# A decoder block on one core: five edits to the order of transfers, products and weight splits

## The chip, the cores and the metric

The kernel runs on one core of one Trainium2 chip. The metric is the device time of one execution in microseconds. The engines are PE (matrix products), DVE, ACT and POOL (vector, scalar and general work), and SP, which here only issues transfers.

## The reference

One decoder block over 1024 tokens of width 1024, in float32. The input is normed (`xn`) and multiplied by `w_in`; the result is cut into a pooling input (512), q, k, v (8 heads of 64 each), an indexer's queries, key and head weights, and two sets of 1024 gates:

```
pooled  = trailing means over 2, 4, 8, 16 tokens minus the token, one window per group of 128
mixed   = (pooled per group @ pool_w) * pool_scale ;  y_pool = mixed @ w_pool_proj
scores  = sum over heads of w * relu(iq . ik), causal ; keep the top 256 keys of each query
o       = softmax attention over the kept keys (q, k with partial rope) ;  y_attn = o @ w_attn_proj
merged  = sigmoid(g0) * y_pool + sigmoid(g1) * y_attn ;  h = x + merged @ w_out
a, b    = halves of (causal conv of width 3 over (norm(h) @ w_up) + conv_b), 2816 each
out     = norm(h + (silu(a) * b) @ w_down)
```

## The kernel before, in words

Every float32 product is made of three products of rounded parts: an operand is split into `hi`, a rounded copy (mostly an ACT cast, L48 or L50), and `lo`, the remainder (a subtraction on DVE or POOL, L51), and PE computes hi*hi, hi*lo and lo*hi into one PSUM bank (`mm3`, L85 to L87). A product of 128x128 by 128x512 is PE's unit of work. Tokens are handled in two halves of 512 (`hf`), eight blocks of 128, and input rows in eight chunks `kc` of 128.

Unless a stage is written under `manual_schedule` for an engine, a scheduler orders each engine's instructions by priorities and readiness. Tiles of a pool with the same tag share buffers; pools opened after others close take their space, and an instruction that writes into a reused place waits for the readers of the old tile.

The stages, in order of time:

- **Indexer, gates and pool branch** (`stages`, L187; `pool_branch`, L667). The normed input, transposed and split, is `xT`: two tiles (h and l) for each token half, allocated half 0 first (L195). For each of four groups g the pool branch loads and splits `w_u` and `pool_w`, computes u (48 products), lets DVE form the window sums `s` and the pooled values `pr`, splits them into `ph` and `pl` (one buffer each, L694 and L695; `pl` on POOL), and multiplies them by the mix weights (`pm`, 6 products). The result, split again, goes to DRAM (`mixd`). Eight `gate(c)` with 48 products each follow. The top-k search runs on DVE all the while.
- **q, k, v.** K and Q blocks are projected, roped on DVE, split (`kst`, `qst`) and transposed by PE; then come eight V blocks, which read `xT` last.
- **Attention** (L780 to L908). For units of one block and one head PE, ACT and DVE run in a hand-written order: scores, mask and minimum on DVE, exponentials on ACT, transposes, split of the transposed weights, product with V, evacuation into `ox` (one buffer). Between the units lie the steps of `pool_out` (y_pool, `yp`): it loads `w_pool_proj`, the gates and the four tiles `mx` of mixed values (POOL's queue, L652), one chunk and half at a time. When a block's last head is done, `finish` (L859) brings the two head halves together: per half one transfer `oy<-ox` moves 64 partitions to the other 64 (SP's queue, L871) and one POOL addition forms `ot` (L872); then POOL adds `oy`, multiplies by the reciprocal sums and writes `oT` hi and lo. POOL's queue also issues the loads of q (`qA`, `qB`, L779 to L781).
- **attn_out** (L910). For each half, for each of eight output chunks: load and split `w_attn_proj[c]` (so each chunk's weights twice), load the gate and the pool result, 12 products `ya`, gate and add on DVE, split into `merged`. PE isn't ordered by hand here: the first products with `w_out` (`wo0p`) fill in.
- **mixer_out** (L926), products with `w_out`, residual, norm, transposes into `x2T`.
- **ffn_up** (L983). 22 chunks c of 128 a-columns and 128 b-columns. `plain(c)` (L1027) makes a chunk with 96 products. `pair(c)` (L1092) makes it with seven products of combined quarters, 84 in all, which need the combinations T1 to T4 of the input; DVE forms them (28 operations of 512 columns in each of `sums_1_2` and `sums_3_4`) beside chunks 1 and 2. Chunks 0 to 2 are plain, 3 to 21 pairs. In `plain` the low halves of the b-columns are POOL's (L1033); in `pair` POOL makes the four weight combinations (L1105) and one low half (L1116). `gated` (L1007) runs the convolution on ACT and DVE, and POOL multiplies the two halves (L1019) and issues the store of 512 KB `gd` (L1021).
- **Down-projection and last norm**, untouched.

Of the kernel before, what the change touches and what calls it, by code (L numbers as in the profile page):

```python
# [9 lines left out]
F32 = mybir.dt.float32  # L10
# [5 lines left out]
ALU = mybir.AluOpType  # L16
# [14 lines left out]
NIDX = 584  # L31
WINDOWS = (2, 4, 8, 16)
# [7 lines left out]
class K:  # L40
# [59 lines left out]
    def weights(self, pool, src, shape, tag, name, eng=None, raw_bufs=1, first=None):  # L100
# [4 lines left out]
        hi = pool.tile(shape, F32R, tag=tag + "h", name=name + "h")  # L105
        lo = pool.tile(shape, F32R, tag=tag + "l", name=name + "l")
        self.split(raw, hi, lo, eng, first)
        return hi, lo
# [78 lines left out]
    def stages(self):  # L187
# [7 lines left out]
        xT = [[xt_pool.tile([P, KC, HB], F32R, name=f"xT{n}{hf}") for n in "hl"] for hf in range(2)]  # L195
        self.xT = [list(t) for t in zip(*xT)]
# [19 lines left out]
        self.pool_branch(mx, pl)  # L216
        close()
        ring, close_ring = self.open("ring", "left", bufs=2)
        for c in range(KC):
            self.gate(c)  # L220
# [446 lines left out]
    def pool_branch(self, cd, pool):  # L667
# [3 lines left out]
        nc.sync.dma_start(self.icnt, io["icnt"])  # L671
        for g, w in enumerate(WINDOWS):
# [21 lines left out]
            ph = pool.tile([P, S], F32R, tag="ph", name=f"ph{g}", bufs=1)  # L694
            pl = pool.tile([P, S], F32R, tag="pl", name=f"pl{g}", bufs=1)  # L695
            self.split(pr, ph, pl, gp)
            for hf in range(2):
                cs = slice(hf * HB, (hf + 1) * HB)
                pm = self.bank("mm", f"pm{g}_{hf}")
                self.mm3(pm, pwh, pwl, ph[:, cs], pl[:, cs], True, True)  # L700
                hi, lo = (cd.tile([P, HB], F32R, tag=f"mixed{n}", name=f"mixed{n}{g}{hf}") for n in range(2))
                nc.scalar.activation(hi, pm, AF.Copy, scale=self.psc[:, g:g + 1])
                nc.vector.scalar_tensor_tensor(lo, pm, self.psc[:, g:g + 1], hi.bitcast(F32),
                                               op0=ALU.mult, op1=ALU.subtract)
                nc.sync.dma_start(self.mixd[0, hf, :, g, :], hi.bitcast(F32))
                nc.sync.dma_start(self.mixd[1, hf, :, g, :], lo.bitcast(F32))
# [61 lines left out]
    def attention(self, pool, fq, yp):  # L768
# [90 lines left out]
        def finish(i):  # L859
# [9 lines left out]
            for o in range(2):  # L869
                mine, other = slice(o * DH, (o + 1) * DH), slice((1 - o) * DH, (2 - o) * DH)  # L870
                nc.sync.dma_start(oy[mine], ox[other, :, o, 0:P])  # L871
                nc.gpsimd.tensor_tensor(ot[mine], ox[mine, :, o, 0:P], ox[mine, :, o, P:2 * P], op=ALU.add)  # L872
# [37 lines left out]
    def attn_out(self, pool):  # L910
        nc, io = self.nc, self.io
        xh, xl = [[self.oT[n][:, :, hf * HB:(hf + 1) * HB] for hf in range(2)] for n in range(2)]
        for hf in range(2):
            for c in range(KC):
                cs = slice(hf * HB, (hf + 1) * HB)
                wh, wl = self.weights(pool, io["w_attn_proj"][c], [P, 4, P], "wa", f"wa{c}_{hf}", raw_bufs=3)
                g1 = pool.tile([P, HB], F32, tag="g1", name=f"g1l{c}_{hf}", bufs=3)
                nc.sync.dma_start(g1, self.g[KC + c][:, cs])
                m0 = pool.tile([P, HB], F32, tag="m0", name=f"m0l{c}_{hf}", bufs=3)
                nc.sync.dma_start(m0, self.m0[c][:, cs])  # L920
                ps = self.fm_half("mm", f"ya{c}_{hf}", wh, wl, xh, xl, 4, hf)
                nc.vector.tensor_tensor(g1, ps, g1, op=ALU.mult)
                nc.vector.tensor_tensor(m0, m0, g1, op=ALU.add)
                self.split(m0, self.merged[hf][0][:, c, :], self.merged[hf][1][:, c, :])
# [58 lines left out]
    def ffn_up(self, fw, pool, wx, x2_last, close_h):  # L983
# [19 lines left out]
        def halves(t, src, eng):  # L1003
            nc.scalar.copy(t[:, 0], src)  # L1004
            eng.tensor_tensor(t[:, 1], src, t[:, 0].bitcast(F32), op=ALU.subtract)  # L1005

        def gated(c, H):  # L1007
# [11 lines left out]
            nc.gpsimd.tensor_tensor(b, a, b, op=ALU.mult)  # L1019
# [67 lines left out]
        with self.tc.manual_schedule(engines=PE):  # L1087
            plain(1, sums_1_2)
            plain(2, sums_3_4)
        T = {n: [t[:, 0], t[:, 1]] for n, t in T.items()}  # L1090

        def pair(c):  # L1092
# [23 lines left out]
            operand_of(4, A[1, 1], nc.gpsimd)  # L1116
# [30 lines left out]
        with self.tc.manual_schedule(engines=PE):  # L1147
            for c in range(3, NF):
                pair(c)
# [305 lines left out]
```

## Time and profile before

| | us |
|---|---|
| median of three runs | 1511.73 (1511.61 to 1514.7) |
| profiled execution | 1508.14 |
| its span, first to last instruction | 1506.4 |
| mean granted TensorE clock | 0.981 |

[...] In the table by stage (rows 3 below) the columns are: the stretch, its length, busy us with the number of instructions for PE, PEld (weight loads), DVE, ACT and POOL, the granted clock, the busy share of the 16 DMA engines, and GB/s. Attention lies from 508.9 to 681.1, attn_out from 686 to 752, the first four chunks of the up-projection from 842 to about 930. In a timeline "[6.25 <-DMA mx<-mixd]" means that the engine was idle for 6.25 us before the instruction and that this transfer ended it. A product of 128x512 is shown with 0.39 us although the next begins earlier: products are pipelined, so PE's rate is read from the distance of starts.

### The profile page before, as it was taken

What the parts mean: (1) busy time and instruction counts of PE and PEld (TensorE: products, weight loads), DVE (VectorE), ACT (ScalarE), POOL (GpSimd) and SP (SyncE); (2) the same over time, 40 slices, a digit from 0 to 9 for tenths busy, and PEclk for the clock granted to TensorE, in tenths of its full rate; (3) what the DMA queues carried; (4) which work ended last, traced back from release to release, by engine and by line L of the source; (5) the groups of instructions that cost most, each with busy time, mean ns of one, the idle gap of its engine ahead of it and who ended that gap; (6) DMA issues with size and microseconds to landing.
All of it is one profiled execution on the core that took longest, in us unless ns stands there. A gap on an engine that the chain in (4) does not pass through costs nothing.

```text
span 1506.4 us, 18703 instructions
## 1 busy us (share of the span) xinstructions
PE 1421.1 (94%) x6682; PEld 1176.5 (78%) x6682; DVE 1151.2 (76%) x1909; ACT 650.0 (43%) x1117; POOL 487.2 (32%) x358
## 2 busy tenths in 40 slices
PE   5999999999889799998899997999999999999997
PEld 4888877887678578886688786888888888888886
DVE  7756999999981156786716878888888888949897
ACT  7656222213333255883402444444444445444353
POOL 4102423213342255534300247555555553100000
PEclk9999999999989899999999998999999999999999
DMA  9002513422013465217621213222222221875663
GB/s 339 15 22 69 161 63 107 140 77 70 29 56 112 161 195 168 71 29 240 228 112 78 93 70 126 85 84 84 84 84 98 84 85 42 306 281 182 239 200 126
DMA packets 74061, 184.46 MB, mean 122 GB/s; under 512 B 8560, under 2 KB 13552, under 8 KB 73456
## 3 DMA queue, kind: packets, MB, share of 16 engines
q1 hardware_dynamic: 65360, 159.16, 30.5%
q0 software_dynamic: 8608, 24.12, 4.7%
q8 instruction: 52, 0.85, 0.2%
q14 instruction: 41, 0.34, 0.1%
HBM read 140.25 MB, written 40.89 MB: 120 GB/s over the span
## 4 chain that ended last, share of the span: by engine, by line
PE 62%; DVE 24%; DMA 5%; issue 3%; ACT 3%; POOL 2%; SPq 0%; ACTq 0%; DVEq 0%; POOLq 0%
DVE tk_junk L563 11%; PE up L85 8%; PE up L87 8%; PE up L86 8%; PE d L87 5%; PE d L86 5%; PE d L85 5%; PE o L844 2%; PE pt L827 2%; DVE tk_r L575 1%; DVE tk_cand L576 1%; PE is L448 1%; PE is L447 1%; PE wvp L87 1%; PE wvp L85 1%
## 5 line engine op out<-in xcount | busy, mean ns | idle before, releaser
L563 DVE TENSOR_SCALAR_CACHE_REDUCE tk_junk<-score,tk_cand 128x384 bf16<-128x384 f32 (+1 forms) x186 | 175.1, 941 | 1.8
L1014 DVE SCALAR_TENSOR_TENSOR acc<-H,cw,acc 128x1023 f32<-128x1023 f32 x88 | 133.2, 1530 | 20.7 <-ACT acc L1012 19.9
L85 PE MATMUL up<-T,w 128*128 128x512 f32 x304 | 118.6, 390 | 0.3 <-ACT w L1004 0.3
L87 PE MATMUL up<-T,w 128*128 128x512 f32 x304 | 118.4, 389 | 0.1
L86 PE MATMUL up<-T,w 128*128 128x512 f32 x304 | 118.3, 389 | 0.0
L85 PE MATMUL d<-op 128*128 128x512 f32 x292 | 113.6, 389 | 0.0
L86 PE MATMUL d<-op 128*128 128x512 f32 x292 | 113.6, 389 | 0.0
L87 PE MATMUL d<-op 128*128 128x512 f32 x292 | 113.6, 389 | 0.0
L1005 DVE TENSOR_TENSOR w<-s,w 128x512 fp32r<-128x512 f32 x76 | 89.4, 1178 | 26.1 <-ACT w L1004 25.8
L1019 POOL TENSOR_TENSOR acc<-acc,acc 128x1024 f32<-128x1024 f32 x22 | 69.8, 3173 | 93.2 <-ACT w L1004 59.7
L1005 POOL TENSOR_TENSOR w<-upr,w 128x512 fp32r<-128x512 f32 x25 | 43.6, 1748 | 135.4 <-DVE w L1005 97.4
L85 PE MATMUL up<-x2T,w 128*128 128x512 f32 x200 | 79.4, 397 | 5.5 <-ACT r L1127 3.2
L1004 ACT CAST w<-s 128x512 fp32r<-128x512 f32 x76 | 47.2, 621 | 80.7 <-PE up L87 80.6
L87 PE MATMUL up<-x2T,w 128*128 128x512 f32 x200 | 79.1, 395 | 0.0
L86 PE MATMUL up<-x2T,w 128*128 128x512 f32 x200 | 79.0, 395 | 0.0
L834 DVE TENSOR_TENSOR PT<-pt,PT 128x512 fp32r<-128x512 f32 (+3 forms) x96 | 50.5, 554 | 29.9 <-ACT PT L833 29.3
L1012 ACT ACTIVATE acc<-H,cb,cw 128x1024 f32<-128x1024 f32 x44 | 54.8, 1245 | 36.8 <-DVE H L1144 23.0
L85 PEld LDWEIGHTS up<-T,w 128*128 128x128 f32 x304 | 57.2, 188 | 12.5 <-ACT w L1004 0.8
L87 PEld LDWEIGHTS up<-T,w 128*128 128x128 f32 x304 | 57.1, 188 | 12.5 <-DVE w L1005 0.5
L1004 ACT CAST w<-upr 128x512 fp32r<-128x512 f32 x69 | 42.1, 618 | 56.9 <-PE up L87 47.5
L86 PEld LDWEIGHTS up<-T,w 128*128 128x128 f32 x304 | 57.2, 188 | 11.9
L85 PEld LDWEIGHTS d<-op 128*128 128x128 f32 x292 | 54.8, 188 | 11.5
(862 smaller groups left out, 4171.8 us busy)
## 6 DMA issues: line engine op xcount, KB each, us to landing
upr<-w_up SPq DMA_DIRECT2D x44, 512.0 KB, 4.1
rawg<-gd SPq DMA_DIRECT2D x37, 512.0 KB, 5.5
raww<-w_down SPq DMA_DIRECT2D x33, 512.0 KB, 5.3
gd<-acc POOLq DMA_DIRECT2D x22, 512.0 KB, 3.1
g<-gt SPq DMA_DIRECT2D x32, 256.0 KB, 2.0
xb<-x SPq DMA_DIRECT2D x8, 512.0 KB, 5.6
xTr<-xT SPq DMA_DIRECT2D x8, 512.0 KB, 6.6
mixd<-mixed SPq DMA_DIRECT2D x16, 256.0 KB, 3.0
```

Source lines behind the costliest of these rows:

```text
L85: t.matmul(ps, sh, mh, start=start, stop=False, skip_group_check=onto)
L86: t.matmul(ps, sh, ml, start=False, stop=False, skip_group_check=onto)
L87: t.matmul(ps, sl, mh, start=False, stop=stop, skip_group_check=onto)
L563: nc.vector.tensor_scalar(junk[:, :W], self.score[b], thr, None, op0=ALU.is_ge, op1=ALU.add, accum_out=cnt[:, j:j + 1])
L827: nc.tensor.transpose(pt[:, j - j0, :], t[:, j * P:(j + 1) * P], self.ident)
L834: nc.vector.tensor_tensor(PT[:, j0:j1, 1, :], pt[:, 0:j1 - j0, :], PT[:, j0:j1, 0, :].bitcast(F32), op=ALU.subtract)
L844: nc.tensor.matmul(live[k]["o"][:, h % 2, :], self.V[:, j, h, :], live[k]["PT"][:, j].rearrange("p a t -> p (a t)"), start=j == 0, stop=j ...
L1004: nc.scalar.copy(t[:, 0], src)
L1005: eng.tensor_tensor(t[:, 1], src, t[:, 0].bitcast(F32), op=ALU.subtract)
L1012: nc.scalar.activation(a, H[o], AF.Identity, bias=cb[:, n:n + 1], scale=cw[:, n, 2:3])
L1014: nc.vector.scalar_tensor_tensor(a[:, d:], H[o][:, 0:S - d], cw[:, n, 2 - d:3 - d], a[:, d:], op0=ALU.mult, op1=ALU.add)
L1019: nc.gpsimd.tensor_tensor(b, a, b, op=ALU.mult)
```

## The change

Five edits:

- `xT` is allocated half 1 first.
- The pool branch becomes a generator: the mix of group g is issued after u of group g+1, the last one after `gate(0)`; `ph` and `pl` get two buffers; PE's order in pool branch and gates is fixed as written.
- `oy<-ox` is issued from POOL's queue.
- `attn_out` runs over pairs of chunks, inside them over halves, inside these over the two chunks; each chunk's weights are loaded and split once and kept (four buffers of hi and lo).
- `PLAIN = 4`: chunk 3 is plain, pairs begin at 4. In plain chunks DVE makes all low halves and the product of the two halves; in the first pair DVE makes the combinations and the low half that were POOL's. The `gd` store stays on POOL's queue.

```diff
-        xT = [[xt_pool.tile([P, KC, HB], F32R, name=f"xT{n}{hf}") for n in "hl"] for hf in range(2)]
-        self.xT = [list(t) for t in zip(*xT)]
+        xT = {hf: [xt_pool.tile([P, KC, HB], F32R, name=f"xT{n}{hf}") for n in "hl"] for hf in (1, 0)}
+        self.xT = [list(t) for t in zip(xT[0], xT[1])]
...
-        self.pool_branch(mx, pl)
-        close()
-        ring, close_ring = self.open("ring", "left", bufs=2)
-        for c in range(KC):
-            self.gate(c)
+        with tc.manual_schedule(engines={mybir.EngineType.PE}):
+            branch = self.pool_branch(mx, pl)
+            next(branch)
+            self.gate(0)
+            for _ in branch:
+                pass
+            close()
+            ring, close_ring = self.open("ring", "left", bufs=2)
+            for c in range(1, KC):
+                self.gate(c)
...
-            ph = pool.tile([P, S], F32R, tag="ph", name=f"ph{g}", bufs=1)
-            pl = pool.tile([P, S], F32R, tag="pl", name=f"pl{g}", bufs=1)
+            ph = pool.tile([P, S], F32R, tag="ph", name=f"ph{g}", bufs=2)
+            pl = pool.tile([P, S], F32R, tag="pl", name=f"pl{g}", bufs=2)
             self.split(pr, ph, pl, gp)
...
+            mixed.append((g, pwh, pwl, ph, pl))
+            if g:
+                mix(*mixed.pop(0))
+        yield
+        mix(*mixed.pop(0))
...
-                nc.sync.dma_start(oy[mine], ox[other, :, o, 0:P])
+                nc.gpsimd.dma_start(oy[mine], ox[other, :, o, 0:P])
...
-        for hf in range(2):
-            for c in range(KC):
-                cs = slice(hf * HB, (hf + 1) * HB)
-                wh, wl = self.weights(pool, io["w_attn_proj"][c], [P, 4, P], "wa", f"wa{c}_{hf}", raw_bufs=3)
...
+        w = {}
+        for c0 in range(0, KC, 2):
+            for hf in range(2):
+                for c in (c0, c0 + 1):
+                    cs = slice(hf * HB, (hf + 1) * HB)
+                    if hf == 0:
+                        w[c] = self.weights(pool, io["w_attn_proj"][c], [P, 4, P], "wa", f"wa{c}", raw_bufs=3, bufs=4)
+                    wh, wl = w[c]
...
-            nc.gpsimd.tensor_tensor(b, a, b, op=ALU.mult)
+            (nc.vector if c < PLAIN else nc.gpsimd).tensor_tensor(b, a, b, op=ALU.mult)
...
-                    halves(w[o, k], raw[:, o, 4 * k:4 * k + 4], nc.gpsimd if o else nc.vector)
+                    halves(w[o, k], raw[:, o, 4 * k:4 * k + 4], nc.vector)
...
             plain(2, sums_3_4)
+            for c in range(3, PLAIN):
+                plain(c)
...
-                nc.gpsimd.tensor_tensor(t, a, b, op=op)
+                (nc.gpsimd if c > PLAIN else nc.vector).tensor_tensor(t, a, b, op=op)
...
-            operand_of(4, A[1, 1], nc.gpsimd)
+            operand_of(4, A[1, 1], nc.gpsimd if c > PLAIN else nc.vector)
...
-            for c in range(3, NF):
+            for c in range(PLAIN, NF):
                 pair(c)
```

`mix` holds the lines L697 to L706 unchanged. The rest of the kernel is as before.

## Rows read from the trace of the kernel before

**Rows 1.** Part 1 of the page: busy us, share and instructions.

```profile
PE 1421.1 (94%) x6682; PEld 1176.5 (78%) x6682; DVE 1151.2 (76%) x1909; ACT 650.0 (43%) x1117; POOL 487.2 (32%) x358
```

**Rows 2.** Waits of PE: line, releaser: us in total, times, longest.

```profile
PE yp L85 <- DMA mx<-mixd: 6.2, 1, 6.2
PE pm L85 <- ACT ph L50: 5.5, 2, 3.3
PE ya L85 <- ACT wa_0h L50: 5.3, 1, 5.3
PE up L85 <- DVE u L1134: 4.5, 2, 4.1
...
PE up L85 <- ACT r L1127: 3.2, 1, 3.2
```

**Rows 3.** Table by stage, columns as named in the profile section.

```profile
225.00:275.00 50.00, 46.56 (x192) 37.55 (x191) 49.79 (x94) 14.02 (x21) 19.26 (x11) 0.94 0.31 103
...
350.00:434.40 84.40, 71.55 (x338) 57.29 (x336) 83.45 (x185) 29.57 (x55) 38.29 (x26) 0.97 0.17 51
...
508.90:522.20 13.30, 4.86 (x13) 3.56 (x13) 1.26 (x6) 1.80 (x7) 4.83 (x7) 0.62 1.01 381
522.20:681.10 158.90, 152.95 (x977) 133.61 (x975) 110.12 (x252) 112.33 (x265) 78.62 (x88) 1.00 0.40 116
...
700.00:753.00 53.00, 46.33 (x181) 34.02 (x182) 42.63 (x55) 22.85 (x40) 18.49 (x14) 0.97 0.75 247
...
911.00:950.00 39.00, 31.25 (x115) 23.99 (x114) 31.34 (x29) 17.01 (x25) 24.52 (x16) 0.87 0.39 144
950.00:1275.00 325.00, 325.00 (x1435) 269.12 (x1434) 268.96 (x257) 147.19 (x202) 169.72 (x116) 1.00 0.22 80
```

**Rows 4.** Timeline of PE, 506 to 523 us: start, us, instruction, idle before.

```profile
508.63 0.27 PE L800 MATMUL s<-kstack,qB 128*128 128x128 f32 x1
515.15 0.76 PE L85 MATMUL yp<-mx,wph 128*128 128x512 f32 x1 [6.25 <-DMA mx<-mixd]
...
522.24 0.22 PE L799 MATMUL s<-kstack,qA 128*128 128x128 f32 x1
```

**Rows 5.** Timeline of POOL, 430 to 535 us.

```profile
508.81 2.17 POOL L652 DMA_DIRECT2D mx<-mixd  x4 [23.91 <-PE s L800]
```

**Rows 6.** The tile mx: landing of its four transfers, 1 MB each.

```profile
DMA to landing us min/median/max: 6.2/9.9/13.2
```

**Rows 7.** Timeline of DVE and POOL, 835 to 950 us.

```profile
844.02 1.25 DVE L75 TENSOR_TENSOR h7u<-h7u,h7t 128x1 f32<-128x1 f32 x1
...
847.68 0.68 DVE L1005 TENSOR_TENSOR w<-upr,w 128x512 fp32r<-128x512 f32 x1
...
880.66 12.35 POOL L1019 TENSOR_TENSOR acc<-acc,acc 128x1024 f32<-128x1024 f32 x1 [6.69 <-DVE acc L1014]
...
931.48 2.67 POOL L1019 TENSOR_TENSOR acc<-acc,acc 128x1024 f32<-128x1024 f32 x1 [1.87 <-issue]
```

**Rows 8.** Timeline of PE, 672 to 754 us.

```profile
686.40 0.76 PE L85 MATMUL ya<-oT,wa_0h 128*128 128x512 f32 x1 [5.27 <-ACT wa_0h L50]
...
751.83 0.39 PE L85 MATMUL wo0p<-wo0a,merged 128*128 128x512 f32 x1
```

**Rows 9.** Groups by line, DVE, 686 to 753 us: busy us, mean ns.

```profile
L51 DVE TENSOR_TENSOR wa_1l<-wa_1r,wa_1h 128x512 fp32r<-128x512 f32 x8 | 9.6, 1205 | 0.9 <-ACT wa_1h L50 0.9
```

**Rows 10.** DMA issues: queue, count, KB each, median us to landing.

```profile
qB<-qd POOLq DMA_DIRECT2D x32, 128.0 KB, 3.6
...
oy<-ox SPq DMA_DIRECT2D x16, 128.0 KB, 3.2
```

**Rows 11.** The tile qB: issues on POOL, duration ns min/median/max, first and last start.

```profile
L780 POOL DMA_DIRECT2D qB<-qd x16: 523/539/614, 477.8 to 640.1; - x16
```

**Rows 12.** Timeline of PE and POOL, 205 to 290 us.

```profile
220.15 0.39 PE L85 MATMUL u<-xTh,wu2h 128*128 128x512 f32 x1
...
223.64 2.39 POOL L51 TENSOR_TENSOR pl<-pr,ph 128x1024 fp32r<-128x1024 f32 x1 [0.93 <-ACT ph L50]
```

More of the change, by code (lines that the diff above doesn't have):

```diff
@@ L31 @@
 NIDX = 584
+PLAIN = 4
 WINDOWS = (2, 4, 8, 16)
@@ L98, in feature_major, with weights @@
                 t.matmul(ps[:, hf, :], wl[:, kc, :], xh[hf][:, kc, :], start=False, stop=last)
-    def weights(self, pool, src, shape, tag, name, eng=None, raw_bufs=1, first=None):
+    def weights(self, pool, src, shape, tag, name, eng=None, raw_bufs=1, first=None, bufs=2):
         nc = self.nc
@@ L104, in weights @@
         nc.sync.dma_start(raw, src)
-        hi = pool.tile(shape, F32R, tag=tag + "h", name=name + "h")
-        lo = pool.tile(shape, F32R, tag=tag + "l", name=name + "l")
+        hi = pool.tile(shape, F32R, tag=tag + "h", name=name + "h", bufs=bufs)
+        lo = pool.tile(shape, F32R, tag=tag + "l", name=name + "l", bufs=bufs)
         self.split(raw, hi, lo, eng, first)
@@ L671, in pool_branch, with mix @@
         nc.sync.dma_start(self.icnt, io["icnt"])
+        mixed = []
+        def mix(g, pwh, pwl, ph, pl):
+            for hf in range(2):
+                cs = slice(hf * HB, (hf + 1) * HB)
+                pm = self.bank("mm", f"pm{g}_{hf}")
+                self.mm3(pm, pwh, pwl, ph[:, cs], pl[:, cs], True, True)
+                hi, lo = (cd.tile([P, HB], F32R, tag=f"mixed{n}", name=f"mixed{n}{g}{hf}") for n in range(2))
+                nc.scalar.activation(hi, pm, AF.Copy, scale=self.psc[:, g:g + 1])
+                nc.vector.scalar_tensor_tensor(lo, pm, self.psc[:, g:g + 1], hi.bitcast(F32),
+                                               op0=ALU.mult, op1=ALU.subtract)
+                nc.sync.dma_start(self.mixd[0, hf, :, g, :], hi.bitcast(F32))
+                nc.sync.dma_start(self.mixd[1, hf, :, g, :], lo.bitcast(F32))
         for g, w in enumerate(WINDOWS):
@@ L693, in pool_branch @@
                                            op0=ALU.mult, op1=ALU.subtract)
-            ph = pool.tile([P, S], F32R, tag="ph", name=f"ph{g}", bufs=1)
-            pl = pool.tile([P, S], F32R, tag="pl", name=f"pl{g}", bufs=1)
+            ph = pool.tile([P, S], F32R, tag="ph", name=f"ph{g}", bufs=2)
+            pl = pool.tile([P, S], F32R, tag="pl", name=f"pl{g}", bufs=2)
             self.split(pr, ph, pl, gp)
-            for hf in range(2):
-                cs = slice(hf * HB, (hf + 1) * HB)
[L699 to L706, printed above, removed]
+            mixed.append((g, pwh, pwl, ph, pl))
[3 more added lines that the diff above has]
+        mix(*mixed.pop(0))
     def load_w(self, pool, src, dst, name):
@@ L912, in attn_out @@
         xh, xl = [[self.oT[n][:, :, hf * HB:(hf + 1) * HB] for hf in range(2)] for n in range(2)]
-        for hf in range(2):
-            for c in range(KC):
-                cs = slice(hf * HB, (hf + 1) * HB)
-                wh, wl = self.weights(pool, io["w_attn_proj"][c], [P, 4, P], "wa", f"wa{c}_{hf}", raw_bufs=3)
[L917 to L924, printed above, removed]
+        w = {}
+        for c0 in range(0, KC, 2):
+            for hf in range(2):
+                for c in (c0, c0 + 1):
+                    cs = slice(hf * HB, (hf + 1) * HB)
+                    if hf == 0:
+                        w[c] = self.weights(pool, io["w_attn_proj"][c], [P, 4, P], "wa", f"wa{c}", raw_bufs=3, bufs=4)
+                    wh, wl = w[c]
+                    g1 = pool.tile([P, HB], F32, tag="g1", name=f"g1l{c}_{hf}", bufs=3)
+                    nc.sync.dma_start(g1, self.g[KC + c][:, cs])
+                    m0 = pool.tile([P, HB], F32, tag="m0", name=f"m0l{c}_{hf}", bufs=3)
+                    nc.sync.dma_start(m0, self.m0[c][:, cs])
+                    ps = self.fm_half("mm", f"ya{c}_{hf}", wh, wl, xh, xl, 4, hf)
+                    nc.vector.tensor_tensor(g1, ps, g1, op=ALU.mult)
+                    nc.vector.tensor_tensor(m0, m0, g1, op=ALU.add)
+                    self.split(m0, self.merged[hf][0][:, c, :], self.merged[hf][1][:, c, :])
     def mixer_out(self, pool, r1, hp):
```

## The prediction

> **What bounds the kernel now.** I read the page's busy shares first: TensorE works 94% of the span [rows 1], so only its gaps and its slow stretches can give anything. The waits of PE say who ends those gaps [rows 2], and the table by stage says where they lie and whether the clock fell there [rows 3]. Its last row is the yardstick: in the steady part of the up-projection 1435 products fill 325.00 us, 0.2265 us each at a granted clock of 1.00. Four stages fall short of it: the start of attention (PE busy 4.86 of 13.3 us, clock 0.62), the output products (46.33 of 53, 0.97), the first chunks of the up-projection (31.25 of 39, 0.87), and the two stages beside the top-k search, where DVE is full (49.79 of 50 and 83.45 of 84.4) and PE isn't [rows 3]. The change touches all of these. The profiled execution took 1508.14 us (span 1506.4), 3.6 us under the median of 1511.73; I make the sum against 1508.1 and add 3.6 at the end. A measurement of this kernel can tell about 0.2%, 3 us, from no change.
>
> **A. The two halves of xT change places.** The last product before attention starts at 508.63; then PE waits until 515.15 for the mixed values, once more a little later, runs its first twelve yp products at the lower clock, and goes on with scores at 522.24 [rows 4]. The four transfers of mixed values are issued by POOL at 508.81, after 23.91 us in which it waited for PE, so it had been free since 484.9 [rows 5]. They need 6.2 to 9.9 us to land (minimum and median) [rows 6]. They wait because their tiles, with those of w_pool_proj and of the first gates, take the space of xT's second half, which the last V products still read. Allocated in the other order, that space holds half 0, whose last reader is V block 3 of 8; four blocks of 24 products at 0.2265 follow it, so it is free 21.7 us earlier, and even the median landing fits in twice. Half 1 then lies where the attention output goes, which is written much later. What is late next is the first softmax: scores, exponentials and the split of the last V block had 13 us of cover and then have 2.7. Without the wait 522.24 - 508.9 = 13.3 us become 12 x 0.2265 = 2.7: a gain of 10.6. Bounds: 10.6, and 7 if block 0's exponentials are late. I take **-10.0**.
>
> **B. Four plain chunks, POOL idle beside them.** The fourth chunk is computed with 96 products in place of 84: 12 x 0.2265 = +2.7 on PE. In its place disappears the first pair's stall: PE waits 4.5 on u (4.1 of it once) and 3.2 on r1 [rows 2], and the clock of 0.87 over 39 us costs 0.13 x 39 = 5.1 [rows 3]; together 12.8. Why DVE is late there shows when POOL runs beside it. A one-column DVE operation takes 1.25 us while POOL splits weights, a 512-column one 0.68 alone; POOL's product takes 12.35 us in the middle of DVE's sums and 2.67 later [rows 7]. The edit moves to DVE: two low halves for each of four chunks (8 x 0.68 = 5.4), four products of a and b, five operations of the next pair (3.4), and it drops about nine 512-column operations of the pair replaced (-6.1). No row shows the 1024-column product on DVE: from below twice 0.68, from above POOL's 2.67; I take 1.36 as DVE's own rate, 5.4 for four. DVE gets 8 us more in some 105, where it now has idle time (31.34 busy of 39 [rows 3]), and is spared the operations stretched by POOL. The transfers of the gated product stay on POOL, now behind DVE. The T sums get one chunk more of time (some 21.7 us of PE) before a pair needs them. Ends: -12 (all 12.8 and half the opening stall, less 2.7) and +3 (the stall only moves to the next pair). I take **-8**, a gap of 2 us left.
>
> **C. attn_out two chunks at a time.** From 686.40 to 751.83 PE runs 192 ya and 24 wo0p products [rows 8]: 65.4 us for 216 x 0.2265 = 48.9, 16.5 lost. Removed: eight loads of 256 KB with their SP issues, eight ACT casts, and eight DVE splits, which take 1.2 us here and 0.68 where nothing is beside them [rows 7, 9], together 5.4 to 9.6 of DVE's work; it has 42.63 in 53 us [rows 3]. PE's waits here are mostly for DVE. The half-0 results now come spread over the stage, so the scheduler has less of wo0p to fill gaps with; that work is only moved. The beginning stays: the 5.3 us for the first weight cast [rows 2] may go, but the low part needs DVE and space that block 7 of attention frees, so I count nothing. DVE's saving does not go over to PE in full. Ends: -13 (all but the cold start) and +1. I take a third of the loss, **-5.5**.
>
> **D. Attention's swapped halves go by POOL's queue.** 16 transfers of 128 KB move from SP, where they land in 3.2 us, to POOL; the nearest row is qB, the same size on POOL's queue in the same stage: 3.6 us [rows 10], 0.54 us of POOL each to issue [rows 11]. That is 16 x 0.54 = 8.6 us of POOL, which has 78.62 of 158.9 [rows 3]. POOL's own order puts the second transfer behind the first add (1.28 us), so it goes out 1.2 us later than now, and the block's end and the release of its ox by 1.6. PE runs 152.95 of 158.9 there [rows 3], so there are other products to hide it. SP no longer stands behind attention, and the first weights may be fetched earlier. Ends: -2, and 8 blocks x 1.6 = +13 with nothing hidden. I take **+0.5**.
>
> [...] The rows show 16 qB issues between 523 and 614 ns with DVE busy beside them [rows 11]. [...]
>
> **E. Pool branch in a fixed PE order.** Products of the mix weights come one group later, after the next group's u. Now the scheduler puts them between; PE waits 5.5 for ph in two places [rows 2] and has clock 0.94 in 50 us (3 lost) [rows 3]. With the fixed order m0 follows u1, whose last product ends at about 220.2, while POOL finishes pl at 223.64 + 2.39 = 226.0 [rows 12]: a wait of 5.9. If all four groups did so, 4 x 5.9 = 23.6, less the 5.5, +18. But DVE, not PE, sets the end of k and q: from 350 to 434.4 PE idles 12.85 us beside a full DVE [rows 3], so a delay up to that is absorbed there. Ends: -8 (all waits and slow clock gone) and +18. I take **+1**.
>
> **Sum:** -10.0 - 8 - 5.5 + 0.5 + 1 = -22.0; 1508.1 - 22.0 = 1486.1, and 3.6 more, in terms of the median, **1489.7**. From here on times are medians.
>
> **Rivals.**
> 1. The fixed order's waits aren't absorbed: +18 in place of +1, 1506.7. For it: DVE's own chain leads to ph. Against it: DVE has other work to do meanwhile. Chance 0.14.
> 2. DVE becomes the bound in B and C: the plain chunk costs its 2.7 and C gives 0, so 1511.7 - 10 + 2.7 + 1.5 = 1505.9. For it: DVE at 31.34 of 39 and 42.63 of 53 before it gets POOL's work. Against it: the stretched operations of [rows 7]. Chance 0.14.
> 3. The mixed values don't move: POOL's queue still has something before them that waits for V. Then -22 + 10 = -12, 1499.7. For it: POOL issues in order, and a transfer of q precedes them. Against it: POOL was idle for 23.91 us with nothing else to wait for [rows 5]. Chance 0.07.
> 4. **Slower:** POOL's queue starves in attention. If issues beside DVE stretch as POOL's product does [rows 7], 12.35 / 2.67 = 4.6 times, each goes from 0.54 to 2.5, two per block are 3.9 more, with the 1.6 of D 5.5 per block, 44 in eight; 1489.7 + 44 - 0.5 = 1533. It decides from 22.5 / 8 = 2.8 us per block that PE really waits. For it: the block's ox has one buffer. Against it: [rows 11]. [...] Chance 0.09.
> Two of the first three together come out near no change: 0.06. The forecast as summed, 1480 to 1497, has 0.50.
>
> **Numbers.** Faster: 0.50 + 0.14 + 0.14 + 0.07 = 0.85; same 0.06; slower 0.09. The low end takes C at -11 and B at -12, about 12 under the forecast, 1478; the high end takes in rivals 1 to 3, 1507. Outside lie the slower case, the middle and a little below.
>
> **What would show it.** A: the mixed values issued about 487, no PE gap near 509, the clock 1.00 there. B: no wait on u or r1, one chunk more of plain products, POOL without operations before the first pair but the transfers of gd, DVE's 512-column operations at 0.7 throughout. C: eight loads of w_attn_proj, the stage nearer 60 than 65 us. D: sixteen oy on POOL's queue landing at about 3.6, PE's wait on ox still near 3. E: waits on pl after u1, u2 and u3, and the k and q stages ending near 434. I am wrong if PE's waits move to ox, if k's end slides past 440, or if the first yp still waits for its transfer.

## The result, and the profile after

The changed kernel takes 1491.06 us (median of four executions, 1490.35 to 1494.92) beside 1511.67 for the kernel before on the same chip: ratio 0.9868, 95% interval 0.9843 to 0.9892. That is 20.6 us less; 1489.7 was forecast.

The profiled execution after has a span of 1493.2 us, the profiled one before 1506.4. They differ by 13.2, not by 20.6, so the stages have to be read one by one. The table gives, for every kernel of this study, distances in us between starts on PE, each worked out from the tiles' rows of that kernel's trace, which give tenths, so that a distance is good to 0.1: from the start of the span to the first u product; on to the first V product; from the first score product to the scores behind the first yp group; on to the last transpose of the sums (attention); on to the first wo1p product (attn_out and what fills it); from the first up product to the first down product. The stretches left out are the same within 0.4 us (V 45.4, the second half of w_out 52.5), but for the end (219.3 to 220.4).

| kernel | start to u | u to V | first yp | attention | attn_out | up | span |
|---|---|---|---|---|---|---|---|
| before | 198.4 | 264.5 | 13.9 | 158.7 | 109.0 | 444.7 | 1506.4 |
| changed | 203.2 | 270.0 | 3.2 | 158.1 | 106.8 | 434.6 | 1493.2 |
| e1_noE | 203.7 | 264.0 | 3.2 | 157.5 | 105.7 | 433.4 | 1484.8 |
| e2_noC | 202.4 | 268.8 | 3.2 | 159.7 | 109.0 | 433.7 | 1495.1 |
| e3_noD | 203.8 | 270.0 | 3.2 | 159.3 | 104.0 | 433.7 | 1491.6 |
| e4_Aonly | 198.5 | 264.7 | 3.2 | 158.1 | 109.3 | 444.8 | 1495.9 |
| e5_plain3 | 198.4 | 268.9 | 3.2 | 159.5 | 105.4 | 432.4 | 1485.1 |
| e6_poolon | 198.5 | 269.3 | 3.2 | 157.7 | 107.7 | 437.8 | 1491.5 |
| e7_early | 202.2 | 265.6 | 3.2 | 157.7 | 104.3 | 433.4 | 1483.6 |
| e8_mixlater | 200.7 | 263.7 | 3.2 | 159.8 | 107.1 | 432.2 | 1483.9 |
| e9_best | 202.1 | 264.4 | 3.2 | 157.8 | 104.5 | 432.4 | 1481.5 |
| e10_start | 202.3 | 264.3 | 16.8 | 160.9 | 107.7 | 444.6 | 1513.9 |
| e11_bestnoD | 202.1 | 264.2 | 3.2 | 158.6 | 102.0 | 432.4 | 1479.6 |
| e12_start2 | 201.9 | 263.4 | 3.2 | 160.1 | 103.1 | 432.3 | 1481.2 |

Between the first two lines lie -10.7 at the first yp group, -10.1 in the up-projection, -2.8 in attention and attn_out together, and, against the change, +5.5 between u and V and +4.8 before any line that the change touches. The last is not the change's: e5_plain3 and e6_poolon have all that code and begin with 198.4 and 198.5.

The timeline of the changed kernel answers to [rows 4, 5]:

```profile
497.27 2.17 POOL L660 DMA_DIRECT2D mx<-mixd  x4 [2.06 <-PE wvp L89]
...
518.86 0.27 PE L817 MATMUL s<-kstack,qB 128*128 128x128 f32 x1
518.97 0.45 PE L87 MATMUL yp<-mx,wph 128*128 128x512 f32 x1
...
521.77 0.22 PE L816 MATMUL s<-kstack,qA 128*128 128x128 f32 x1
```

POOL now waits for a V product in the middle of that stage, 21.6 us ahead of the last score product; PE goes from it to yp without a gap, and the twelve products take 2.80 us, from 518.97 to 521.77, at a granted clock of 1.00.

The table by stage for the first chunks of the up-projection. First a line of the kernel before, which goes with the sixth of [rows 3]:

```profile
840.00:911.00 71.00, 67.92 (x297) 55.49 (x296) 59.95 (x83) 33.24 (x53) 32.17 (x12) 0.98 0.17 61
```

Then the same two stretches of the changed kernel:

```profile
840.00:911.00 71.00, 71.00 (x307) 58.32 (x306) 63.59 (x97) 35.47 (x55) 1.48 (x2) 0.96 0.23 83
911.00:950.00 39.00, 39.00 (x174) 32.30 (x173) 24.10 (x26) 15.61 (x24) 13.01 (x10) 1.00 0.26 95
```

PE is full in both, at a clock of 1.00 (the profile gives it as a share of full speed) in the second, where it had 31.25 busy at 0.87; DVE is busy for 63.59 + 24.10 = 87.7 us in the two stretches, before 59.95 + 31.34 = 91.3, although it has taken over POOL's part; POOL does almost nothing in the first. The stretches don't hold quite the same work: the changed up-projection begins 3.2 us earlier and has no pair at chunk 3. The comparison with the same chunks is that of e6_poolon, below.

The waits of PE, changed kernel:

```profile
PE pm L87 <- ACT ph L52: 6.9, 3, 3.3
PE pm L88 <- POOL pl L53: 6.6, 4, 1.9
PE ya L89 <- DVE wa0l L53: 4.6, 1, 4.6
...
PE up L87 <- DVE u L1157: 0.4, 1, 0.4
```

Against [rows 2] the waits for mx and r1 are gone and that for u is 0.4; the mix products now wait 13.5 us in place of 5.5; and the wait at the start of attn_out has only changed its name, from the first cast (the high part of the weights) to their first low part.

### The profile page after: what moved, and what is told of

The parts are those of the page before. It is cut to its first block, busy times and chain, and to the rows that moved or that the text cites. A ratio compares the mean times of both kernels' runs of the same rounds, so it can differ in the third digit from the quotient of the medians.

```text
span 1493.2 us, 18608 instructions
## 1 busy us (share of the span) xinstructions
PE 1418.0 (95%) x6694; PEld 1177.1 (79%) x6694; DVE 1137.0 (76%) x1909; ACT 646.0 (43%) x1108; POOL 446.7 (30%) x354
## 4 chain that ended last, share of the span: by engine, by line
PE 68%; DVE 22%; DMA 3%; ACT 3%; issue 3%; POOL 1%; SPq 0%; ACTq 0%; DVEq 0%; POOLq 0%
DVE tk_junk L571 11%; PE up L87 9%; PE up L88 9%; PE up L89 9%; PE d L87 5%; PE d L88 5%; PE d L89 5%; PE o L861 2%; PE pt L844 2%; DVE tk_r L583 2%; DVE tk_cand L584 1%; PE is L456 1%; PE is L455 1%; PE wvp L87 1%; PE wvp L88 1%
## 5 line engine op out<-in xcount | busy, mean ns | idle before, releaser
L1035 DVE SCALAR_TENSOR_TENSOR acc<-H,cw,acc 128x1023 f32<-128x1023 f32 x88 | 129.4, 1484 | 15.8 <-ACT acc L1033 15.1
L87 PE MATMUL up<-T,w 128*128 128x512 f32 x288 | 112.0, 389 | 0.0
L88 PE MATMUL up<-T,w 128*128 128x512 f32 x288 | 112.0, 389 | 0.0
L89 PE MATMUL up<-T,w 128*128 128x512 f32 x288 | 112.0, 389 | 0.0
L1026 DVE TENSOR_TENSOR w<-s,w 128x512 fp32r<-128x512 f32 x72 | 82.5, 1146 | 34.8 <-ACT w L1025 34.5
L87 PE MATMUL up<-x2T,w 128*128 128x512 f32 x208 | 82.4, 396 | 2.3 <-ACT w L1025 2.3
L88 PE MATMUL up<-x2T,w 128*128 128x512 f32 x208 | 82.1, 395 | 0.0
L89 PE MATMUL up<-x2T,w 128*128 128x512 f32 x208 | 82.1, 395 | 0.0
L1040 POOL TENSOR_TENSOR acc<-acc,acc 128x1024 f32<-128x1024 f32 x18 | 49.2, 2733 | 80.8 <-ACT w L1025 52.2
L1042 POOL DMA_DIRECT2D gd<-acc x22 | 16.4, 747 | 161.2 <-DVE acc L1040 160.3
L89 PEld LDWEIGHTS d<-op 128*128 128x128 f32 x292 | 54.8, 188 | 11.5
L87 PEld LDWEIGHTS d<-op 128*128 128x128 f32 x292 | 54.8, 188 | 11.5
L88 PEld LDWEIGHTS d<-op 128*128 128x128 f32 x292 | 54.8, 188 | 11.2
L87 PEld LDWEIGHTS up<-T,w 128*128 128x128 f32 x288 | 54.1, 188 | 11.3
```

Source lines behind the costliest of these rows:

```text
L87: t.matmul(ps, sh, mh, start=start, stop=False, skip_group_check=onto)
L88: t.matmul(ps, sh, ml, start=False, stop=False, skip_group_check=onto)
L89: t.matmul(ps, sl, mh, start=False, stop=stop, skip_group_check=onto)
L1035: nc.vector.scalar_tensor_tensor(a[:, d:], H[o][:, 0:S - d], cw[:, n, 2 - d:3 - d], a[:, d:], op0=ALU.mult, op1=ALU.add)
L1040: (nc.vector if c < PLAIN else nc.gpsimd).tensor_tensor(b, a, b, op=ALU.mult)
```

## The experiments

All edits are against the changed kernel unless said otherwise. Times are medians, ratios are to executions of the kernel before on the same chip, whose median was 1510.2 to 1512.4. The kernels ran on several chips, so between chips the ratios are compared and not the medians; most intervals overlap, and it is the distances in the table that tell the edits apart. "..." in a diff marks lines left out.

**e1_noE.** Pool branch and gates as before:

```diff
-        with tc.manual_schedule(engines={mybir.EngineType.PE}):
-            branch = self.pool_branch(mx, pl)
...
+        self.pool_branch(mx, pl)
+        close()
+        ring, close_ring = self.open("ring", "left", bufs=2)
+        for c in range(KC):
+            self.gate(c)
...
```

The lines left out put the mix back into its group, with one buffer each for ph and pl.

> The changed kernel with pool branch and gates as before (no fixed order of PE, mix weights in the same group). Theory 1: the fixed order costs; in the two profiles the stretch from the first u product to the first V product is 264.5 us before and 270.0 after, so it goes back to 264 to 265, and the median falls by 4 to 6 from 1491 to about 1486. Rival: DVE's top-k search sets the end of the stretch and the 5.5 us belong to that one execution, which started late; then the stretch differs by less than 2 and the median stays within 2 of 1491. My forecast had +1 for this part.

Measured: 1487.06, ratio 0.9836 (0.9815 to 0.9857), u to V 264.0. The fixed order costs: in the five kernels that have it as the change made it the stretch is 268.8 to 270.0, in the eight with the order of before 263.4 to 265.6.

**e2_noC.** `attn_out` as before:

```diff
-        w = {}
-        for c0 in range(0, KC, 2):
-            for hf in range(2):
-                for c in (c0, c0 + 1):
...
+        for hf in range(2):
+            for c in range(KC):
...
+                wh, wl = self.weights(pool, io["w_attn_proj"][c], [P, 4, P], "wa", f"wa{c}_{hf}", raw_bufs=3)
...
```

> The changed kernel with attn_out as before: two passes, weights loaded and split twice. Theory 1: from the transposes of the last block's sums to the first wo1p product it was 109.4 us before and 107.2 after, so the part is worth about 2: 1493. Rival, my forecast: 5.5, so 1496 to 1497. A third: the gain of 2 comes from SP's freedom and not from this part; then the stretch stays at 107 and the time at 1491.

Measured: 1497.09, ratio 0.9898 (0.9877 to 0.9919); attn_out 109.0, exactly what it was. The third theory is out. The stretch is 2.2 longer and the median 6 higher; the medians can't tell 2 from 5, and the next run shows that the size depends on the queue of the oy transfers.

**e3_noD.** The transfers back on SP:

```diff
-                nc.gpsimd.dma_start(oy[mine], ox[other, :, o, 0:P])
+                nc.sync.dma_start(oy[mine], ox[other, :, o, 0:P])
```

> The changed kernel with the oy transfers back on SP's queue. Theory 1: attention's stretch is 0.5 us longer (158.2 against 157.7) and the first products of attn_out, which began 4 us earlier after attention, begin later again, but the first product with the low part stays at 7.2 us after the last transposes, since its split waits for ox either way: 1491 to 1492. Rival: the early fetch of weights is worth its 4 us: 1495. Second rival, the slower case of my forecast: POOL's queue costs in attention, and without it the stretch is shorter by 3 or more: 1488 or less.

Measured: 1492.91, ratio 0.987 (0.9848 to 0.9893): no difference from the change. But inside, attention is 1.2 longer and attn_out 2.8 shorter, 104.0, the first product with a low part again at the same distance from the last transposes (6.7 against 6.8). The timeline of PE at the start of attn_out, changed kernel first:

```profile
681.41 0.47 PE L87 MATMUL ya<-oT,wa0h 128*128 128x512 f32 x1 [1.28 <-ACT wa0h L52]
...
686.69 0.79 PE L89 MATMUL ya<-oT,wa0l 128*128 128x512 f32 x1 [4.58 <-DVE wa0l L53]
```

and e3_noD:

```profile
687.25 0.77 PE L87 MATMUL ya<-oT,wa0h 128*128 128x512 f32 x1 [5.30 <-ACT wa0h L52]
```

With SP free the first product comes 4 us earlier (681.41 is 1.6 us after the last transpose, with SP's queue it is 5.6), but PE gets only two products out of it and then waits 4.58 for the low part. With SP's queue PE waits 5.30 once.

**e4_Aonly.** The kernel before with the halves of xT exchanged and nothing else:

```diff
-        xT = [[xt_pool.tile([P, KC, HB], F32R, name=f"xT{n}{hf}") for n in "hl"] for hf in range(2)]
-        self.xT = [list(t) for t in zip(*xT)]
+        xT = {hf: [xt_pool.tile([P, KC, HB], F32R, name=f"xT{n}{hf}") for n in "hl"] for hf in (1, 0)}
+        self.xT = [list(t) for t in zip(xT[0], xT[1])]
```

> The kernel before with only the two halves of xT exchanged. Theory 1: from the first score product to the second group of scores it takes 3.2 us in place of 13.9, and the whole gains that, 10.7: 1511.7 becomes 1501. Rival: part of it comes back as waits in attention for the first softmax or for later gates, and the median is 1503 to 1506. Second rival: the gain needs POOL's or SP's queue as in the whole change, and the mixed values still come late: 1511.

Measured: 1497.88, ratio 0.9913 (0.9894 to 0.9931), 14.5 under the kernel before; first yp 3.2, nothing given back in attention (158.1). This edit alone carries over half of the change. The median falls by more than the 10.7 of the two profiles. A possible reason, not shown by a run of its own, is in e10_start, which lacks the edit too and whose profiled execution was the slowest of its twelve: there the first yp group took 16.8 us. Without the edit the wait depends on how long four transfers of 1 MB take (6.2 to 13.2 us in the kernel before, 8.3 to 15.2 in e10_start); with it they take 6.3 to 14.7 and the distance is 3.2 in all twelve traces.

**e5_plain3.** `PLAIN = 4` becomes `PLAIN = 3`, DVE keeps POOL's work.

> The changed kernel with pairs from chunk 3 again, but DVE still does the work of POOL in plain chunks and in the first pair. From the first up product to the first down product it took 444.7 us before and 434.6 changed. Theory 1: the stretch is mostly DVE stretched by POOL, so without POOL the pair at chunk 3 is nearly free of waits, and the 12 products of the plain chunk (2.7 us) are saved: 432 to 435, median 1489 to 1491. Rival: the fourth plain chunk gives the sums the time they need; without it the pair waits as before, and the stretch is 440 or more, median 1496 or more.

Measured: 1488.01, ratio 0.9861 (0.9837 to 0.9885), up 432.4, the shortest but for e8_mixlater's 432.2, and the same in e9, e11 and e12, which have it too. The wait for u is 1.5 us there, so some of the pair's stall is left. With four plain chunks and DVE doing POOL's work, six traces have 432.2 to 434.6. The fourth plain chunk isn't needed; whether its 12 products more cost anything beyond a microsecond isn't settled.

**e6_poolon.** Four plain chunks, POOL works as before:

```diff
-            (nc.vector if c < PLAIN else nc.gpsimd).tensor_tensor(b, a, b, op=ALU.mult)
+            nc.gpsimd.tensor_tensor(b, a, b, op=ALU.mult)
...
-                    halves(w[o, k], raw[:, o, 4 * k:4 * k + 4], nc.vector)
+                    halves(w[o, k], raw[:, o, 4 * k:4 * k + 4], nc.gpsimd if o else nc.vector)
...
-                (nc.gpsimd if c > PLAIN else nc.vector).tensor_tensor(t, a, b, op=op)
+                nc.gpsimd.tensor_tensor(t, a, b, op=op)
...
```

> The changed kernel with four plain chunks, but the low halves, the product of the halves and the combinations on POOL as before. Theory 1 (POOL stretches DVE): part of the wait comes back at the first pair, the stretch from first up to first down product is 438 to 445, median 1494 to 1501. Rival: the fourth plain chunk alone hides it, 434 to 436 and 1491.

Measured: 1493.66, ratio 0.9898 (0.9875 to 0.992), up 437.8, just under the range of theory 1. Either half of the edit takes most of the stall (-6.9 this one, -12.3 the other). What POOL does to DVE shows in the groups by line between 840 and 950 us (busy us, mean ns of one), changed kernel:

```profile
L1026 DVE TENSOR_TENSOR w<-upr,w 128x512 fp32r<-128x512 f32 x21 | 14.8, 721 | 2.0 <-ACT w L1025 2.0
...
L1040 DVE TENSOR_TENSOR acc<-acc,acc 128x1024 f32<-128x1024 f32 x4 | 4.9, 1219 | 0.0
```

and e6_poolon:

```profile
L1026 DVE TENSOR_TENSOR w<-upr,w 128x512 fp32r<-128x512 f32 x10 | 14.3, 1434 | 6.0 <-ACT w L1025 6.0
...
L1040 POOL TENSOR_TENSOR acc<-acc,acc 128x1024 f32<-128x1024 f32 x4 | 21.4, 5352 | 20.1 <-DVE acc L1035 10.8 <-issue 9.4
```

The same product takes 1.22 us on DVE and 5.35 on POOL, and half as many splits keep DVE busy as long: 1.43 us each in place of 0.72. In the 110 us from the first up product DVE is busy for 90.9 us in e6_poolon, with 104 instructions, and for 87.7 in the changed kernel, with 124.

**e7_early.** e1_noE, and in attn_out the first weights ahead of all gate loads, each chunk's tiles in a place of their own:

```diff
+        def fetch(c):
+            w[c] = self.weights(pool, io["w_attn_proj"][c], [P, 4, P], f"wa{c % 4}", f"wa{c}", raw_bufs=1, bufs=1)
+
+        fetch(0)
+        fetch(1)
...
+                    if hf == 0 and c + 2 < KC:
+                        fetch(c + 2)
```

> Pool branch and gates as before (1487 us so far), and in attn_out the first two chunks' weights are fetched and split before any gate load, each chunk's raw, high and low tiles in a place of their own. In the changed kernel the first weights' low part waits for attention's last transfer (PE waits 4.58), and the second chunk's fetch stands in SP's queue behind a gate load that waits for the same place. Theory 1: with both gone, the first product with a low part comes 1 to 2 us after the last transposes, in place of 6.8, and the median falls by 3 to 6, to 1481 to 1484. Rival: the oT of block 7 (ready near 690) and the gate loads hold PE anyway, the stretch to the first wo1p product stays within 1 us of 105.7, and the time at 1487.

Measured: 1486.26, ratio 0.9835 (0.9805 to 0.9864); attn_out 104.3 against 105.7. The low part does come early, 3.2 us after the last transpose in place of 6.8, and a wait appears one step on, first on PE, then what DVE does at that time:

```profile
688.64 0.76 PE L87 MATMUL ya<-oT,wa0h 128*128 128x512 f32 x1 [4.96 <-DVE g1l L935]
```

```profile
687.20 0.69 DVE L53 TENSOR_TENSOR wa3l<-wa3r,wa3h 128x512 fp32r<-128x512 f32 x1 [2.96 <-ACT wa3h L52]
687.81 0.68 DVE L935 TENSOR_TENSOR g1l<-ya,g1l 128x512 f32<-128x512 f32 x1
```

PE runs two half chunks and then stands 4.96 us until DVE has taken the first result out of its PSUM bank. What DVE waits for isn't the gate, whose load was issued at 603.27 and landed at 607.21: in DVE's order the split of chunk 3's weights stands before that operation, and it waits 2.96 us for its cast. So the early fetch of later weights holds up the first result; the same fetch behind the gating wasn't tried. The gain is 1.4, nearer the rival.

**e8_mixlater.** The fixed order, mix products later still:

```diff
             next(branch)
             self.gate(0)
+            self.gate(1)
+            next(branch)
+            self.gate(2)
...
+            if g >= 2:
+                mix(*mixed.pop(0))
             ph = pool.tile([P, S], F32R, tag="ph", name=f"ph{g}", bufs=2)
...
```

The mix weights also get a third buffer, since they are kept longer.

> The changed kernel with the mix products still later in PE's fixed order: u0, u1, u2, mix 0, u3, mix 1, two gates, mix 2, a gate, mix 3. Theory 1: what costs in the fixed order is that ph and pl aren't ready when the mix comes (PE waits 13.5 on them); two groups later they are, PE waits under 3 on them, and the stretch from the first u to the first V product falls from 270.0 to 260 to 264; median 1482 to 1487. Rival: DVE's top-k and ropes set the end of k and q: the waits move to the transposes of k and q, and the stretch stays at 264 or above, the median at 1486 to 1491.

Measured: 1486.88, ratio 0.9842 (0.9819 to 0.9866), u to V 263.7. A wait of PE in this kernel:

```profile
PE k0t L150 <- POOL kst L53: 3.8, 1, 3.8
```

and one in e1_noE, with the scheduler's order:

```profile
PE pm L87 <- ACT ph L52: 6.6, 3, 4.0
```

No product waits for ph or pl any more (the mix products wait 3.6 us in all, for DVE to read out the ones before them), and yet the stretch is what it was with 6.6 of such waits: 3.8 appear at the first k transposes, and the waits at q1t (3.9) and k7t (3.5) are the same in both kernels. So about 264 is a floor that doesn't come from the mix products, and a mix later still wins nothing against the scheduler's order; the change's order overruns the floor by 5.

**e9_best, e11_bestnoD.** e7_early with `PLAIN = 3`; the first also with the low half of the first gate's weights on DVE (below), the second with oy on SP's queue instead.

> What the runs so far favour, together: the halves of xT exchanged, pairs from chunk 3 with POOL's work on DVE, attn_out in pairs of chunks with the first weights early, oy on POOL's queue, pool branch and gates as before; and the low half of the first gate's weights, which POOL makes at about 12 us, on DVE. From 1487 (pool branch as before) less 1 (pairs from chunk 3) less 1.6 (early weights) = 1484. Theory on the start: DVE's one-column operation there takes 2.0 to 2.3 us in place of 0.16 whenever POOL's subtraction has begun just before it, and the stretch up to the first u is then 200.7 to 203.8 in place of 198.4; with nothing on POOL it is 198.4 to 200 in every execution, so 1480 to 1482. Rival: DVE's own 1.3 us for that split, ahead of the first xT, delay as much: 1484 to 1485.

> As the first kernel of this call, but with the oy transfers on SP's queue and the first gate's split on POOL. Theory 1: the transfers' queue matters little in attention (157.5 to 159.5 us either way), but SP's queue then holds the first weights behind the last block's transfers, so the first product with a low part comes 2 to 4 us later: 1485 to 1488. Rival: on POOL the transfers cost; 1483 or less.

Measured: 1483.32, ratio 0.981 (0.9787 to 0.9832), and 1480.61, ratio 0.9801 (0.9778 to 0.9825): both beat the kernel before, and the second is the fastest found, some 10 us under the changed kernel. Its theory 1, 1485 or more with SP's queue, failed; the first lies between its theory and its rival. SP's queue again gives a shorter attn_out, 102.0 against 104.5, though the first product with a low part comes 4 us later (7.3 against 3.2 after the last transpose).

**e10_start, e12_start2.** Where the executions scatter: up to the first u the traces have 198.4 to 198.5 or 200.7 to 203.8, and the eleven kernels other than e9, e10 and e12 have the same code there. The timeline of DVE and POOL shows why, changed kernel first:

```profile
11.77 2.34 POOL L53 TENSOR_TENSOR wg8l<-wg8r,wg8h 128x1024 fp32r<-128x1024 f32 x1 [10.00 <-ACT wg8h L52]
11.80 2.32 DVE L81 TENSOR_TENSOR a03y<-a03y,a03t 128x1 f32<-128x1 f32 x1
```

and the kernel before:

```profile
11.80 0.16 DVE L79 TENSOR_TENSOR a03y<-a03y,a03t 128x1 f32<-128x1 f32 x1
...
12.10 2.35 POOL L51 TENSOR_TENSOR wg8l<-wg8r,wg8h 128x1024 fp32r<-128x1024 f32 x1 [10.34 <-ACT wg8h L50]
```

The same one-column operation takes 0.16 us, or 2.32 when POOL's subtraction begins 0.03 us ahead of it. Of the eleven traces six show it so, with 2.00 to 2.32 us and POOL 0.03 to 0.39 ahead, and in each the operation ends within 0.03 us of the end of the subtraction; the copy of 128 columns behind it then takes 1.25 in place of 0.23, beside POOL's next split. In e8_mixlater the copy alone is caught, with 2.40 us, and the first u comes at 200.7; the four traces without either begin with 198.4 or 198.5. e10_start is the kernel before with that one split on DVE, e12_start2 is e11_bestnoD with the next one (the index key's) on DVE as well:

```diff
-        return self.weights(self.ws, self.io["w_gate"][c], [P, KC, P], "w", f"wg{c}", self.nc.gpsimd)
+        return self.weights(self.ws, self.io["w_gate"][c], [P, KC, P], "w", f"wg{c}",
+                            self.nc.vector if c == KC else self.nc.gpsimd)
...
-                self.split(wikr, wk[:, :, 0], wk[:, :, 1], nc.gpsimd)
+                self.split(wikr, wk[:, :, 0], wk[:, :, 1], nc.vector)
```

> The kernel before with only the low half of the first gate's weights moved from POOL to DVE. Theory: the executions of the kernel before scatter from 1507 to 1515 because in some of them POOL's subtraction at 12 us comes just before DVE's small operations; without it the stretch up to the first u is 198.4 to 200, the median falls by 1 to 3 from 1511, and the executions lie within 2 us. Rival: the scatter has another cause; then the median stays at 1510 to 1512 with the same scatter, or rises by the 1.3 us of DVE's work.

> The fastest kernel so far (xT's halves exchanged, pairs from chunk 3 without POOL, attn_out in pairs with early weights, oy on SP's queue, pool branch as before: 1480.6, executions from 1478.6 to 1485.7), with both weight splits that POOL makes at 12 to 15 us, the first gate's and the index key's, on DVE. Theory of the start: DVE's one-column operations took 1.04 to 2.3 us beside POOL's subtractions; with POOL empty there they take 0.2, the stretch to the first u is that of the undisturbed executions plus DVE's own 1.9 us, so at most 200.5, where this kernel had 202.1, and the executions lie closer together: median 1479 to 1481. Rival: the operations stay long, or the stretch stays at 202 or more with DVE's added work: 1480 to 1483.

Measured: 1508.94, ratio 0.9992 (0.9978 to 1.0005), executions 1506.2 to 1515.7; and 1482.94, ratio 0.9809 (0.9788 to 0.983). Neither gains beyond the noise: e10_start is 1.5 us under the kernel before on its chip, with an interval that holds 1 and with the scatter of before where its theory had 2 us, and e12_start2 stays at 201.9 to the first u, above the 200.5 that its theory allowed. That POOL stretches the operation is confirmed, with POOL empty it is short again:

```profile
14.17 0.15 DVE L81 TENSOR_TENSOR a03y<-a03y,a03t 128x1 f32<-128x1 f32 x1
```

but it starts at 14.17 in place of 11.80, behind DVE's own two splits. That is 2.4 of the 3.5 us by which its first u comes after 198.4; where the rest arises wasn't followed up. With one split moved (e10_start) POOL's other one still caught it (1.04 us). A remedy would have to delay POOL's work without giving it to DVE; that wasn't tried.

## Why the prediction was right, point by point

The total was met, 1491.06 against 1489.7, but single terms were off in opposite directions, A and B better than forecast by 2.8 together, D and E worse by 5 to 6, so that the nearness of the total is partly luck. Like parts compared, from the table (the interval of the whole is 16.3 to 23.7 us):

| part | forecast | measured | from |
|---|---|---|---|
| A | -10.0 | -10.7 | e4_Aonly against before |
| B | -8 | -10.1 | changed against before |
| C | -5.5 | -5.0 | e3_noD (104.0) against before (109.0), both with oy on SP; with oy on POOL -2.2, changed against e2_noC |
| D | +0.5 | about +1.6 | changed against e3_noD: -1.2 and +2.8 |
| E | +1 | +5 to +6 | changed and four more against those without |
| sum | -22.0 | -18.2 to -19.2 | |

The 3.6 us that I added for the median need a word too: the profiled execution before began with the undisturbed 198.4 us to the first u, so it stood below its own median, as said; the profiled one after had 203.2 and stands above its median by 3.9. Span against span would have shown only 13.2. The low end of the range was added up wrongly: C at -11 and B at -12 lie 9.5 under the forecast, not 12, at 1480.

- **A** went as worked out: space, reader, landing. The mixed values are issued at 497.27 and not about 487, as this execution started 4.8 us late and E added 5.5. The first softmax was not late: the second score product follows the twelfth yp product at once.
- **B**: the mechanism, DVE stretched by POOL (1.43 us for a split in e6_poolon, 0.72 in the changed kernel), was right and undersized by 2 us: no gap of 2 us is left at the first pair. That DVE is relieved although it gets more work is in the table by stage. The 1.36 us taken for DVE's product are 1.22. One argument of the step fell: that the sums need a fourth plain chunk. e5_plain3 is as fast without it, so the 2.7 us that the chunk costs PE bought nothing.
- **C**: the size was right with SP's queue, where the part gives 5.0; in the change it shows as 2.2, and D gives back the rest in the same stretch. The 5.0 rests on one trace, and with oy on POOL attn_out scatters from 105.4 to 107.7 without a further edit to it. No run separates the saved loads, casts and splits.
- **D**: the forecast sought the cost in attention and the gain at the start of attn_out. It is the other way round: attention is shorter, if anything (mean 158.5 in the eight kernels with POOL's queue, 159.3 in the six with SP's), and the early start of attn_out brings nothing, since PE then waits for the low part. Why attn_out is 2 us longer with it is not settled: after its wait PE is slow in both cases (a product is shown with 0.77 and 0.79 us in the two timelines and the ones behind it start 0.43 apart; in the changed kernel the granted clock was 0.50 from 686.69 to 690.00), and the waits differ in several places. The slower rival, POOL's issues stretched beside DVE, did not come: oy's issues took 0.617 to 0.699 us in the changed kernel, the four of them with DVE idle 0.62 to 0.65 and the twelve beside an operation of DVE 0.62 to 0.70, and the transfers landed in 3.0 (median of 16) against 3.2 on SP's queue [rows 10]. The operations beside them were subtractions, one product with a gate and the custom minimum with its accumulator read; for others nothing is shown. What the traces do show is operations stretched while one of the other engine ran: on DVE 0.16 and 2.32 us at the start, the 2.32 beside a subtraction of POOL of 2.34 and ending within 0.03 us of it, and 0.72 and 1.43 for a split in the up-projection.
- **E** is the term that failed. The forecast counted on DVE's full stretch to absorb up to 12.85 us of delay. The first operation of the first k block's rope on DVE, in the kernel before and in the changed one, with its start behind the three durations:

```profile
L119 DVE TENSOR_TENSOR k0ra<-k,cos x1: 288/288/288, 355.1 to 355.1; 128x128 f32<-128x128 f32 x1
```

```profile
L121 DVE TENSOR_TENSOR k0ra<-k,cos x1: 278/278/278, 369.3 to 369.3; 128x128 f32<-128x128 f32 x1
```

  Since the changed execution started 4.8 us late, times have to be counted from the first u: k's first rope comes 9.4 us later than before (166.1 against 156.7), q3's rope 2.3 later (249.2 against 246.9) and the first V product 5.5 later, while the top-k search's last operation starts 2.1 earlier (241.4 against 243.5). So of 9.4 us of delay some 4 are absorbed and 5.5 are left: PE's idle time from 160 us after the first u to the first V product falls from 12.8 us to 8.0 and no further. Most of the delay comes from the mix products: m0 waited 3.30 and 1.64, 4.9 in place of the forecast 5.9, and the waits for ph and pl came to 13.5, 8.0 more than before. The floor of 264 us is real (e8_mixlater), and it fits DVE: in the nine kernels with 263 to 266 us DVE is idle for 3.2 us between the first u and q3's rope, in the five with 269 to 270 for 6.1, which fits PE being late there. No run made DVE's work shorter to show the floor move. Rival 1 had the mechanism and too high a price.

The condition that I gave for being wrong in E, k's end past 440, was a poor one: k's last transposes began at 428.47 (414.58 before) and the part was still too long by 5. The k and q stages did not end near 434 either: in the kernel before that is where q1's transposes begin (434.38), in the changed one they begin at 446.97, and q3's follow.

## What to carry to other kernels

When a transfer at a stage's border is late, look first whose space it waits for: here the order of two allocations was worth as much as the rewriting of the first up-projection chunks. Before an order of products is fixed by hand, find the engine that sets the stage's end, and test the order against the scheduler's: here the fixed order lost 5 us, or with the mix later still came out even. And an engine that takes work off another one isn't free if the two stretch each other (a split on DVE 0.72 and 1.43 us in the changed kernel and e6_poolon, the product on POOL 12.35 and 2.67 in the kernel before [rows 7]); with POOL's share of the work back on DVE the up-projection got 3 us shorter (434.6 against 437.8 in e6_poolon).

## What the runs showed of the hardware that was not expected

An operation of one column on DVE, 0.16 us, took 2.32 when a subtraction of POOL had started 0.03 us before it. In the two profiles of the change that order turned on a load of weights: ACT's cast waited for it and began at 10.64 us in the changed kernel and at 10.97 in the one before, and DVE's operation at 11.80 in both. The first u product moves by 2 to 5 us with it: 198.4 or 198.5 us in four of the traces, 200.7 to 203.8 in the ten others (three of these with DVE's own splits there). A single profiled execution can so be off by as much as C, D or E is worth, and stage distances told the parts apart where medians couldn't.
